# Two-layer hybrid trunk: the FFN up-projections take both activation parts behind one weight part

## The chip, the cores and the metric

The kernel runs on one core of one Trainium2 chip. The metric is the time of the program on the device in microseconds (us): the median of several runs. One more run is profiled; its trace gives the start and length of every instruction on the engines: TensorE (PE, and PEld for its weight loads), VectorE (DVE), ScalarE (ACT), GpSimd (POOL), and SyncE (SP), whose queue issues the large transfers.

## The reference

The input x is 256 tokens of 1024 channels in float32. Two layers follow one another, each of three steps:

```python
for l in range(DEPTH):                                   # DEPTH = 2
    x = x + 0.5 * swiglu(rms_norm(x, norm_gain[l, 0]), w_ffn_in[l, 0], w_ffn_out[l, 0])
    x = x + hybrid_mixer(rms_norm(x, norm_gain[l, 1]), ...)
    x = x + 0.5 * swiglu(rms_norm(x, norm_gain[l, 2]), w_ffn_in[l, 1], w_ffn_out[l, 1])

def swiglu(h, w_in, w_out):
    gate, up = jnp.split(h @ w_in, 2, axis=-1)           # 1024 -> 2 x 2816
    return (jax.nn.silu(gate) * up) @ w_out              # 2816 -> 1024
```

So there are four feed-forward networks (FFNs) and two mixers. The mixer (four kinds of attention, gates and an output projection) is not touched.

## The kernel before, in words

**Precision.** Every large product is made from split operands. A float32 weight is split into a high part (whi, a cast on ACT, line 187) and the rest (wlo, a subtraction on VectorE or, in a few places, on GpSimd, line 188), both in the type fp32r. The activations are split the same way; their two parts are hh and hl. A product is then three matmuls (mm3, lines 192 to 194): high by high, high by low, low by high.

**An FFN.** Its 2816 gate columns and 2816 up columns are done in 11 blocks j of 256 and 256. Blocks 0 and 1 go through up_first, where the tokens are stationary. Blocks 2 to 10 go through up(j, rv): the weight is stationary and the 256 tokens stream. In up, c counts the two halves of 128 columns, g is 0 for gate and 1 for up, and the 8 steps k run over the 1024 channels. One k-step is one mm3. For one c, the gate goes into the first 256 columns of a PSUM bank pm and the up values into the other 256. Then line 288 multiplies the whole bank by rb (the inverse norm of each token, in all partitions), line 291 takes SiLU of the gate half, line 293 multiplies, and lines 295 and 296 split the result into act for the down product.

After up(j) follow the down products of the rows m = 2j-4 and 2j-3: 12 matmuls of 512 columns for each m, into four accumulators that stay in PSUM over the FFN. The last four m are done in join, which also begins the next part of the layer (its norm, its first splits and transposes, the latter into banks pt).

**Order.** Raw weights come by SP's queue in tiles of 1 MB (five buffers) and are split into eight pairs of buffers in turn ("wide"); a split waits until its pair is free. The order of the instructions on each engine is set by a scheduler, which simulates the program, except in join, where it is fixed by hand, and for a few transfers that keep their place. One thing falls into the first FFN alone: setup, called behind block 3, builds the table of position biases (ld, then rep, 4 MB, then bias), with three transfers that stand in SP's queue among the weight loads.

Of the kernel before, what the change touches and what calls it, by code (L numbers as in the profile page):

```python
# [9 lines left out]
F32 = mybir.dt.float32  # L10
F32R = mybir.dt.float32r
AF = mybir.ActivationFunctionType
ALU = mybir.AluOpType
# [55 lines left out]
def tile_trunk(ctx: ExitStack, tc: tile.TileContext, a: dict, out: bass.AP):  # L69
# [49 lines left out]
    def norm(l, n):  # L119


        hh = h_p.tile([128, KC, T], F32R, name="hh", tag="hh")
        hl = h_p.tile([128, KC, T], F32R, name="hl", tag="hl")
        rs = sm.tile([128, 16], F32, name="rt", tag="rt", bufs=2)
        rb = wk.tile([128, T], F32, name="rb", tag="rb", bufs=1)

        def main(i):
            xg = []
            for q in range(2):
                ps = pt.tile([128, 4, 128], F32, name="pt", tag="pt")  # L130
                for c in range(4):
                    nc.tensor.transpose(ps[:, c, :], x[:, i, (4 * q + c) * 128:(4 * q + c + 1) * 128], ident[:])
                xg.append(wk.tile([128, 4, 128], F32, name="xg", tag="pT"))
                g = gn[:, 3 * l + n, 4 * q:4 * q + 4].rearrange("p (c o) -> p c o", o=1)
                nc.vector.tensor_tensor(xg[q][:], ps[:], g.to_broadcast([128, 4, 128]), op=ALU.mult)
                nc.scalar.copy(hh[:, 4 * q:4 * q + 4, i * 128:i * 128 + 128], xg[q][:])
            for q in range(2):
                o = (slice(None), slice(4 * q, 4 * q + 4), slice(i * 128, i * 128 + 128))
                nc.vector.tensor_tensor(hl[o], xg[q][:], f(hh[o]), op=ALU.subtract)  # L139

        def stats(i):
            ss = sm.tile([128, 16], F32, name="ss", tag="ss")
            for h in range(2):
                junk = wk.tile([128, 512], F32, name="junk", tag="e", bufs=3)
                nc.scalar.activation(out=junk[:], in_=x[:, i, h * 512:(h + 1) * 512], func=AF.Square,
                                     scale=D ** -0.5, accum_out=ss[:, h:h + 1])
            ms = sm.tile([128, 16], F32, name="ms", tag="ms")
            nc.vector.scalar_tensor_tensor(out=ms[:, 0:1], in0=ss[:, 0:1], scalar=EPS, in1=ss[:, 1:2],
                                           op0=ALU.add, op1=ALU.add)
            nc.gpsimd.tensor_tensor(rs[:, i:i + 1], ms[:, 0:1], neg_half[:, 0:1], op=ALU.pow)  # L150

        def rows():
            for i in range(NT):
                dg = wk.tile([128, 128], F32, name="dg", tag="av")
                nc.vector.tensor_scalar(out=dg[:], in0=ident[:], scalar1=rs[:, i:i + 1], scalar2=None, op0=ALU.mult)
                ps = pt.tile([128, 128], F32, name="pt", tag="pt")
                nc.tensor.matmul(ps[:], lhsT=ones[:], rhs=dg[:], start=True, stop=True)
                nc.scalar.copy(rb[:, i * 128:(i + 1) * 128], ps[:])

        return main, stats, (hh, hl, rs, rb, rows)  # L160

    def raw_tile(name="raw"):
        return raw_p.tile([128, 2048], F32, name=name, tag="raw")
# [27 lines left out]
    def mm3(ps, lh, ll, rh, rl, start, stop):  # L191
        nc.tensor.matmul(ps, lhsT=lh, rhs=rh, start=start, stop=False)  # L192
        nc.tensor.matmul(ps, lhsT=lh, rhs=rl, start=False, stop=False)  # L193
        nc.tensor.matmul(ps, lhsT=ll, rhs=rh, start=False, stop=stop)  # L194

    pinned = (mybir.EngineType.PE, mybir.EngineType.Activation, mybir.EngineType.DVE)

# [17 lines left out]
    def ffn(l, s, nxt=None, aside=None):  # L215
# [62 lines left out]

        def up(j, rv):
            for c in range(2):  # L280
                ps = pm.tile([128, 2, T], F32, name="pm", tag="pm")
                for g in range(2):
                    wh, wl = split(rv[g][:, :, c * 128:(c + 1) * 128], wide)
                    for k in range(KC):
                        mm3(ps[:, g, :], wh[:, k, :], wl[:, k, :], hh[:, k, :], hl[:, k, :],
                            k == 0, k == KC - 1)
                z = wk.tile([128, 2, T], F32, name="z", tag="pT")
                nc.vector.tensor_tensor(z[:], ps[:], rb[:].rearrange("p (o t) -> p o t", o=1)  # L288
                                        .to_broadcast([128, 2, T]), op=ALU.mult)
                sl = wk.tile([128, T], F32, name="sl", tag="sl")  # L290
                nc.scalar.activation(out=sl[:], in_=z[:, 0, :], func=AF.Silu)
                av = wk.tile([128, T], F32, name="av", tag="av")
                nc.vector.tensor_tensor(av[:], z[:, 1, :], sl[:], op=ALU.mult)
                ah, al = pair_tile()
                nc.scalar.copy(ah, av[:])  # L295
                nc.gpsimd.tensor_tensor(al, av[:], f(ah), op=ALU.subtract)  # L296
# [27 lines left out]
        w0, todo = first(0)  # L324
        w1, more = first(1)
        todo += more
        hh, hl, rs, rb, rows = yield todo
        yield from up_first(0, w0)
        rows()
        acc01 = pa.tile([128, 2, 512], F32, name="acc01", tag="a01")  # L330
# [121 lines left out]
    def mixer(l, nxt):  # L452
# [38 lines left out]
        g0, g1 = weights(804, 512, wide, (0, 1, 2, 3)), weights(0, 384, wide)  # L491
        w0, w1 = [], []
        todo = [lambda: w0.append(next(g0))] * 4 + [lambda: w1.append(next(g1))] * 4
        hh, hl, rt, rb, rows = yield todo
        ps0 = tiles()
        for i in range(NT):
            for e in range(4):
# [518 lines left out]
```

## Time and profile before

| what | value |
|---|---|
| median of 3 runs | 1394.11 us (1391.5 to 1396.48) |
| the profiled execution | 1394.26 us |
| its span, first to last instruction | 1392.5 us |
| granted TensorE clock, mean | 0.998 |
| PE busy | 1358.7 us, 98% |
| DVE busy | 875.7 us, 63% |
| ACT busy | 676.4 us, 49% |
| POOL busy | 265.0 us, 19% |
| chain that ended last, by engine | PE 91%, DVE 5%, ACT 2% |

How to read it: the share of PE says that TensorE does nearly all of the time; what an edit is worth is then how much it shortens the row of matmuls, less what it makes TensorE wait. The length shown for one matmul (0.28 us for 256 columns) covers its way through the pipeline; matmuls overlap, so their cost is the distance from one start to the next.

### The profile page before, as it was taken

What the parts mean: (1) busy time and instruction counts of PE and PEld (TensorE: products, weight loads), DVE (VectorE), ACT (ScalarE), POOL (GpSimd) and SP (SyncE); (2) the same over time, 40 slices, a digit from 0 to 9 for tenths busy, and PEclk for the clock granted to TensorE, in tenths of its full rate; (3) what the DMA queues carried; (4) which work ended last, traced back from release to release, by engine and by line L of the source; (5) the groups of instructions that cost most, each with busy time, mean ns of one, the idle gap of its engine ahead of it and who ended that gap; (6) DMA issues with size and microseconds to landing.
All of it is one profiled execution on the core that took longest, in us unless ns stands there. A gap on an engine that the chain in (4) does not pass through costs nothing.

```text
span 1392.5 us, 23262 instructions
## 1 busy us (share of the span) xinstructions
PE 1358.7 (98%) x9393; PEld 1254.2 (90%) x9393; DVE 875.7 (63%) x1498; ACT 676.4 (49%) x1052; POOL 265.0 (19%) x209
## 2 busy tenths in 40 slices
PE   7999999999999999999999999999999999999998
PEld 7998989879988989999999999898789989899997
DVE  6545646687587676555475555567866977765552
ACT  6424535646444555444454444355554555554441
POOL 0111232240022040111301111322300312211110
PEclk9999999999999999999999999999999999999999
DMA  9549733545343366555555555354543424665530
GB/s 348 173 157 372 252 118 120 186 149 180 122 143 101 122 213 210 182 182 182 182 177 187 182 182 197 95 168 156 182 136 122 152 91 146 212 209 190 183 122 31
DMA packets 173597, 237.10 MB, mean 170 GB/s; under 512 B 5085, under 2 KB 144545, under 8 KB 173489
## 3 DMA queue, kind: packets, MB, share of 16 engines
q1 hardware_dynamic: 172275, 235.16, 50.9%
q8 instruction: 74, 1.21, 0.3%
q10 hardware_dynamic: 1182, 0.38, 0.1%
q14 instruction: 34, 0.28, 0.1%
q0 software_dynamic: 32, 0.07, 0.0%
HBM read 234.51 MB, written 5.21 MB: 172 GB/s over the span
## 4 chain that ended last, share of the span: by engine, by line
PE 91%; DVE 5%; ACT 2%; issue 1%; DMA 1%; POOL 0%; SPq 0%; ACTq 0%; DVEq 0%; POOLq 0%
PE pm L192 17%; PE pm L194 17%; PE pm L193 17%; PE acc L192 6%; PE acc L193 6%; PE acc L194 6%; PE zp L193 4%; PE zp L194 4%; PE zp L192 4%; PE ov L586 2%; DVE wlo L188 2%; PE pt L579 1%; PE sl L811 1%; PE xo L194 1%; PE xo L193 1%
## 5 line engine op out<-in xcount | busy, mean ns | idle before, releaser
L188 DVE TENSOR_TENSOR wlo<-raw,whi 128x1024 fp32r<-128x1024 f32 (+3 forms) x426 | 514.6, 1213 | 275.1 <-ACT whi L187 272.9
L187 ACT CAST whi<-raw 128x1024 fp32r<-128x1024 f32 (+5 forms) x446 | 452.1, 1020 | 467.5 <-PE pm L193 293.8
L192 PE MATMUL pm<-hh,whi 128*128 128x256 f32 x1664 | 473.1, 284 | 3.2 <-ACT whi L187 1.9
L194 PE MATMUL pm<-hh,wlo 128*128 128x256 f32 x1664 | 472.6, 284 | 0.8 <-DVE wlo L188 0.8
L193 PE MATMUL pm<-hl,whi 128*128 128x256 f32 x1664 | 471.7, 283 | 0.0
L192 PEld LDWEIGHTS pm<-hh,whi 128*128 128x128 f32 x1664 | 317.1, 191 | 9.0 <-issue 4.6
L194 PEld LDWEIGHTS pm<-hh,wlo 128*128 128x128 f32 x1664 | 317.2, 191 | 2.9 <-issue 1.3
L193 PEld LDWEIGHTS pm<-hl,whi 128*128 128x128 f32 x1664 | 317.4, 191 | 1.7 <-issue 0.3
L296 POOL TENSOR_TENSOR act<-av,act 128x256 fp32r<-128x256 f32 x72 | 96.0, 1333 | 543.6 <-ACT act L295 539.2
L192 PE MATMUL acc<-whi,act 128*128 128x512 f32 x352 | 138.3, 394 | 0.0
L193 PE MATMUL acc<-wlo,act 128*128 128x512 f32 x352 | 138.2, 393 | 0.0
L194 PE MATMUL acc<-whi,act 128*128 128x512 f32 x352 | 137.9, 392 | 0.0
L193 PE MATMUL zp<-wlo,hh 128*128 128x512 f32 (+4 forms) x320 | 115.9, 363 | 1.1 <-DVE wlo L188 1.1
L194 PE MATMUL zp<-whi,hl 128*128 128x512 f32 (+4 forms) x320 | 114.4, 358 | 0.0
L192 PE MATMUL zp<-whi,hh 128*128 128x512 f32 (+4 forms) x320 | 110.1, 361 | 1.2 <-ACT whi L187 1.2
L288 DVE TENSOR_TENSOR z<-pm,rb 128x512 f32<-128x512 f32 x72 | 49.7, 691 | 57.0 <-PE pm L194 56.8
L906 POOL TENSOR_TENSOR yt<-yt,tg 128x512 f32<-128x512 f32 x24 | 40.9, 1725 | 204.7 <-DVE tg L904 198.0
L194 PEld LDWEIGHTS acc<-whi,act 128*128 128x128 f32 x352 | 66.1, 188 | 15.1
L192 PEld LDWEIGHTS acc<-whi,act 128*128 128x128 f32 x352 | 66.1, 188 | 13.3
L193 PEld LDWEIGHTS acc<-wlo,act 128*128 128x128 f32 x352 | 66.2, 188 | 13.1
L114 POOL TENSOR_TENSOR rs<-ms,neg_half 128x4 f32<-128x4 f32 (+3 forms) x44 | 53.5, 1223 | 124.9 <-DVE ms L111 124.9
L194 PE MATMUL pm<-whi,hl 128*128 128x256 f32 x256 | 73.0, 285 | 2.4 <-DVE hl L139 2.4
(189 smaller groups left out, 1790.5 us busy)
## 6 DMA issues: line engine op xcount, KB each, us to landing
raw<-in_w_ffn_in_dram SPq DMA_DIRECT2D x66, 1024.0 KB
raw<-in_w_in_dram SPq DMA_DIRECT2D x52, 1024.0 KB
raw<-in_w_ffn_out_dram SPq DMA_DIRECT2D x44, 1024.0 KB
raw<-in_w_ffn_in_dram SPq DMA_DIRECT2D x44, 512.0 KB
raw<-in_w_branch_dram SPq DMA_DIRECT2D x8, 1024.0 KB
raw<-in_w_out_dram SPq DMA_DIRECT2D x8, 1024.0 KB
raw<-in_w_in_dram SPq DMA_DIRECT2D x8, 768.0 KB
rep<-ld SPq DMA_DIRECT2D x1, 4032.0 KB
```

The source lines that it names most:

```text
L114: nc.gpsimd.tensor_tensor(rs[:, :n], ms[:, :n], neg_half[:, :n], op=ALU.pow)
L187: nc.scalar.copy(hv, src)
L188: (eng or nc.vector).tensor_tensor(lv, src, f(hv), op=ALU.subtract)
L192: nc.tensor.matmul(ps, lhsT=lh, rhs=rh, start=start, stop=False)
L193: nc.tensor.matmul(ps, lhsT=lh, rhs=rl, start=False, stop=False)
L194: nc.tensor.matmul(ps, lhsT=ll, rhs=rh, start=False, stop=stop)
L288: nc.vector.tensor_tensor(z[:], ps[:], rb[:].rearrange("p (o t) -> p o t", o=1) .to_broadcast([128, 2, T]), op=ALU.mult)
L296: nc.gpsimd.tensor_tensor(al, av[:], f(ah), op=ALU.subtract)
L579: nc.tensor.transpose(ps[:, c, :], p[:, (done + c) * 128:(done + c + 1) * 128], ident[:])
L586: nc.tensor.matmul(o[:, h, :], lhsT=pT[:, j, :], rhs=pv(j), start=j == 0, stop=j == nb - 1)
L811: nc.tensor.matmul(p, lhsT=q_of(h)[:, i * 128:(i + 1) * 128], rhs=k_of(h)[:, :n], start=True, stop=True)
L906: nc.gpsimd.tensor_tensor(y, y, t[:], op=ALU.add)
```

## The change

The two activation parts become the two halves of one tile h2. A k-step of up has two matmuls instead of three: the high weight part against both halves of h2 at once (512 columns, a whole bank), and the low weight part against the high half (256 columns, added into the first half of the bank). In the last step of a sum they are issued the other way round, so that the one that writes the whole bank ends it. Gate and up now have a bank each: the gate's from the pool pm, the up values' from the pool pt, which the transposes use as well. The two halves of a bank still have to be added. So for each of the two, the bank is multiplied into z (512 columns) and the halves of z are added (256 columns, both from SBUF). The gate is multiplied by rb, goes through SiLU, and is multiplied by rb again on GpSimd; the product is the factor of the up bank, which gives av.

```diff
--- before.py
+++ after.py
@@ -119,8 +119,8 @@
     def norm(l, n):
 
 
-        hh = h_p.tile([128, KC, T], F32R, name="hh", tag="hh")
-        hl = h_p.tile([128, KC, T], F32R, name="hl", tag="hl")
+        h2 = h_p.tile([128, 2, KC, T], F32R, name="h2", tag="h2")
+        hh, hl = h2[:, 0], h2[:, 1]
         rs = sm.tile([128, 16], F32, name="rt", tag="rt", bufs=2)
         rb = wk.tile([128, T], F32, name="rb", tag="rb", bufs=1)
 
@@ -157,7 +157,7 @@
                 nc.tensor.matmul(ps[:], lhsT=ones[:], rhs=dg[:], start=True, stop=True)
                 nc.scalar.copy(rb[:, i * 128:(i + 1) * 128], ps[:])
 
-        return main, stats, (hh, hl, rs, rb, rows)
+        return main, stats, (h2, rs, rb, rows)
 
     def raw_tile(name="raw"):
         return raw_p.tile([128, 2048], F32, name=name, tag="raw")
@@ -192,6 +192,14 @@
         nc.tensor.matmul(ps, lhsT=lh, rhs=rh, start=start, stop=False)
         nc.tensor.matmul(ps, lhsT=lh, rhs=rl, start=False, stop=False)
         nc.tensor.matmul(ps, lhsT=ll, rhs=rh, start=False, stop=stop)
+
+    def mm2(ps, wh, wl, r2, start, stop):
+
+
+        parts = [lambda: nc.tensor.matmul(ps, lhsT=wh, rhs=r2, start=start, stop=stop),
+                 lambda: nc.tensor.matmul(ps[:, 0], lhsT=wl, rhs=r2[:, 0], start=False, stop=False)]
+        for p in reversed(parts) if stop else parts:
+            p()
 
     pinned = (mybir.EngineType.PE, mybir.EngineType.Activation, mybir.EngineType.DVE)
 
@@ -278,19 +286,27 @@
 
         def up(j, rv):
             for c in range(2):
-                ps = pm.tile([128, 2, T], F32, name="pm", tag="pm")
+                ps = []
                 for g in range(2):
+                    pool, tag = (pm, "pm") if g == 0 else (pt, "pt")
+                    ps.append(pool.tile([128, 2, T], F32, name=tag, tag=tag))
                     wh, wl = split(rv[g][:, :, c * 128:(c + 1) * 128], wide)
                     for k in range(KC):
-                        mm3(ps[:, g, :], wh[:, k, :], wl[:, k, :], hh[:, k, :], hl[:, k, :],
-                            k == 0, k == KC - 1)
-                z = wk.tile([128, 2, T], F32, name="z", tag="pT")
-                nc.vector.tensor_tensor(z[:], ps[:], rb[:].rearrange("p (o t) -> p o t", o=1)
-                                        .to_broadcast([128, 2, T]), op=ALU.mult)
-                sl = wk.tile([128, T], F32, name="sl", tag="sl")
-                nc.scalar.activation(out=sl[:], in_=z[:, 0, :], func=AF.Silu)
-                av = wk.tile([128, T], F32, name="av", tag="av")
-                nc.vector.tensor_tensor(av[:], z[:, 1, :], sl[:], op=ALU.mult)
+                        mm2(ps[g][:], wh[:, k, :], wl[:, k, :], h2[:, :, k, :], k == 0, k == KC - 1)
+
+                def both(g, by, name):
+
+                    z = wk.tile([128, 2, T], F32, name="z", tag="pT")
+                    nc.vector.tensor_tensor(z[:], ps[g][:], by[:].rearrange("p (o t) -> p o t", o=1)
+                                            .to_broadcast([128, 2, T]), op=ALU.mult)
+                    r = wk.tile([128, T], F32, name=name, tag=name)
+                    nc.vector.tensor_tensor(r[:], z[:, 0], z[:, 1], op=ALU.add)
+                    return r
+
+                sl = both(0, rb, "sl")
+                nc.scalar.activation(out=sl[:], in_=sl[:], func=AF.Silu)
+                nc.gpsimd.tensor_tensor(sl[:], sl[:], rb[:], op=ALU.mult)
+                av = both(1, sl, "av")
                 ah, al = pair_tile()
                 nc.scalar.copy(ah, av[:])
                 nc.gpsimd.tensor_tensor(al, av[:], f(ah), op=ALU.subtract)
@@ -324,7 +340,8 @@
         w0, todo = first(0)
         w1, more = first(1)
         todo += more
-        hh, hl, rs, rb, rows = yield todo
+        h2, rs, rb, rows = yield todo
+        hh, hl = h2[:, 0], h2[:, 1]
         yield from up_first(0, w0)
         rows()
         acc01 = pa.tile([128, 2, 512], F32, name="acc01", tag="a01")
@@ -491,7 +508,8 @@
         g0, g1 = weights(804, 512, wide, (0, 1, 2, 3)), weights(0, 384, wide)
         w0, w1 = [], []
         todo = [lambda: w0.append(next(g0))] * 4 + [lambda: w1.append(next(g1))] * 4
-        hh, hl, rt, rb, rows = yield todo
+        h2, rt, rb, rows = yield todo
+        hh, hl = h2[:, 0], h2[:, 1]
         ps0 = tiles()
         for i in range(NT):
             for e in range(4):
```

On TensorE, in the second FFN, at the end of one g and the start of the next in block 2, before:

```order
L192 MATMUL pm_5882<-hh_5526,whi_5883 128x256
L193 MATMUL pm_5882<-hl_5527,whi_5883 128x256
L194 MATMUL pm_5882<-hh_5526,wlo_5884 128x256
L192 MATMUL pm_5882<-hh_5526,whi_5911 128x256
L193 MATMUL pm_5882<-hl_5527,whi_5911 128x256
L194 MATMUL pm_5882<-hh_5526,wlo_5912 128x256
```

and in the changed kernel the end of the first g, and then the start of the second (acc are the accumulators of the down products, act the activations):

```order
L200 MATMUL pm_5681<-h2_5326,wlo_5683 128x256
L199 MATMUL pm_5681<-h2_5326,whi_5682 128x512
L200 MATMUL pm_5681<-h2_5326,wlo_5683 128x256 x2
L199 MATMUL pm_5681<-h2_5326,whi_5682 128x512
L192 MATMUL acc01_5552<-whi_5793,act_5370 128x512
L193 MATMUL acc01_5552<-wlo_5794,act_5370 128x512
L194 MATMUL acc01_5552<-whi_5793,act_5370 128x512
```

```order
L193 MATMUL acc01_5552<-wlo_5810,act_5371 128x512
L281 MATMUL pt_5670<-ident_89,av_5668 128x128 x2
L199 MATMUL pt_5702<-h2_5326,whi_5703 128x512
L200 MATMUL pt_5702<-h2_5326,wlo_5704 128x256
L199 MATMUL pt_5702<-h2_5326,whi_5703 128x512
```

The three matmuls have become two, and in this block, which follows up_first and its transposes, one down product (12 matmuls) and the first two matmuls of the next have moved between the two g. In the later blocks nothing stands between them.

On VectorE, in the second FFN in block 4 (z is a bank times rb or sl; sl and av are the two halves of z added, or av the product of before), before:

```order
L288 TENSOR_TENSOR z_6279<-pm_6222,rb_5529 128x512
L188 TENSOR_TENSOR wlo_6488<-raw_6390,whi_6487 128x1024
L293 TENSOR_TENSOR av_6283<-z_6279,sl_6281 128x256
L188 TENSOR_TENSOR wlo_6527<-raw_6524,whi_6526 128x1024
L288 TENSOR_TENSOR z_6345<-pm_6288,rb_5529 128x512
L188 TENSOR_TENSOR wlo_6543<-raw_6524,whi_6542 128x1024
L293 TENSOR_TENSOR av_6349<-z_6345,sl_6347 128x256
```

and in the changed kernel:

```order
L300 TENSOR_TENSOR z_6019<-pm_5977,rb_5328 128x512
L303 TENSOR_TENSOR sl_6021<-z_6019 128x256
L188 TENSOR_TENSOR wlo_6182<-raw_6121,whi_6181 128x1024
L300 TENSOR_TENSOR z_6025<-pt_5998,sl_6021 128x512
L303 TENSOR_TENSOR av_6027<-z_6025 128x256
L188 TENSOR_TENSOR wlo_6203<-raw_6123,whi_6202 128x1024
L300 TENSOR_TENSOR z_6074<-pm_6032,rb_5328 128x512
L303 TENSOR_TENSOR sl_6076<-z_6074 128x256
L188 TENSOR_TENSOR wlo_6238<-raw_6235,whi_6237 128x1024
L300 TENSOR_TENSOR z_6080<-pt_6053,sl_6076 128x512
```

For each c there are a z and an add more, and one split stands between the first add and the second z, where ACT's SiLU and the product on GpSimd fall.

On SP's queue, in the first FFN (ld, rep and bias are the three transfers of setup; a pair of raw loads from w_ffn_in is one g of a block), before:

```order
L404 DMA ld_788<-line_786 21x384
L409 DMA rep_790<-ld_788 2688x1x384
L233 DMA raw_1202<-in_w_ffn_in_dram 128x4x256 x2
L313 DMA raw_1337<-in_w_ffn_out_dram 128x2x1024
L233 DMA raw_1371<-in_w_ffn_in_dram 128x4x256 x2
L233 DMA raw_1374<-in_w_ffn_in_dram 128x4x256 x2
L411 DMA bias_101<-rep_790 128x21x256
```

and in the changed kernel:

```order
L421 DMA ld_743<-line_741 21x384
L426 DMA rep_745<-ld_743 2688x1x384
L241 DMA raw_1113<-in_w_ffn_in_dram 128x4x256 x2
L329 DMA raw_1226<-in_w_ffn_out_dram 128x2x1024
L241 DMA raw_1260<-in_w_ffn_in_dram 128x4x256 x2
L428 DMA bias_101<-rep_745 128x21x256
L241 DMA raw_1263<-in_w_ffn_in_dram 128x4x256 x2
```

The transfer of bias has moved ahead of the second g of block 7; ld and rep keep their place in the queue.

## Rows read from the trace of the kernel before

**Rows 1.** Page: each engine's busy time with instructions, and the chain by engine.

```profile
PE 1358.7 (98%) x9393; PEld 1254.2 (90%) x9393; DVE 875.7 (63%) x1498; ACT 676.4 (49%) x1052; POOL 265.0 (19%) x209
PE 91%; DVE 5%; ACT 2%; issue 1%; DMA 1%; POOL 0%; SPq 0%; ACTq 0%; DVEq 0%; POOLq 0%
```

**Rows 2.** Page, costliest groups: count | busy us, mean ns | idle before, releaser.

```profile
L192 PE MATMUL pm<-hh,whi 128*128 128x256 f32 x1664 | 473.1, 284 | 3.2 <-ACT whi L187 1.9
```

**Rows 3.** Windows, first and second FFN: us; busy PE PEld DVE ACT POOL; PEclk, DMA, GB/s.

```profile
36.22:126.36 90.14, 87.50 (x613) 80.95 (x611) 47.15 (x66) 35.34 (x52) 9.50 (x9) 1.00 0.63 211
...
537.91:697.79 159.88, 159.88 (x1115) 149.36 (x1114) 86.52 (x94) 69.81 (x94) 34.42 (x22) 1.00 0.56 186
```

**Rows 4.** Timeline of PE, second FFN (start us, us): group starts in up and down.

```profile
555.12 0.28 PE L192 MATMUL pm<-hh,whi 128*128 128x256 f32 x1
...
557.93 0.28 PE L192 MATMUL pm<-hh,whi 128*128 128x256 f32 x1
...
560.81 0.28 PE L192 MATMUL pm<-hh,whi 128*128 128x256 f32 x1
...
566.50 0.40 PE L192 MATMUL acc<-whi,act 128*128 128x512 f32 x1
...
569.25 0.39 PE L192 MATMUL acc<-whi,act 128*128 128x512 f32 x1
...
571.97 0.28 PE L192 MATMUL pm<-hh,whi 128*128 128x256 f32 x1
...
588.94 0.28 PE L192 MATMUL pm<-hh,whi 128*128 128x256 f32 x1
...
600.43 0.40 PE L192 MATMUL acc<-whi,act 128*128 128x512 f32 x1
...
603.24 0.39 PE L192 MATMUL acc<-whi,act 128*128 128x512 f32 x1
...
605.99 0.28 PE L192 MATMUL pm<-hh,whi 128*128 128x256 f32 x1
```

**Rows 5.** Timeline of PE, mixer of layer 0: a plain run of 512 columns.

```profile
207.24 0.39 PE L192 MATMUL zp<-whi,hh 128*128 128x512 f32 x1
...
209.99 0.71 PE L132 MATMUL pt<-ident,x 128*128 128x128 f32 x5
```

**Rows 6.** Groups by line and shape, second FFN, 549.59 to 697.79 us, columns as above.

```profile
L188 DVE TENSOR_TENSOR wlo<-raw,whi 128x1024 fp32r<-128x1024 f32 x47 | 57.6, 1225 | 48.6 <-ACT whi L187 48.6
L187 ACT CAST whi<-raw 128x1024 fp32r<-128x1024 f32 x51 | 53.5, 1049 | 77.2 <-PE pm L193 53.5 <-PE acc L194 21.0 <-PE acc L193 2.6
...
L296 POOL TENSOR_TENSOR act<-av,act 128x256 fp32r<-128x256 f32 x18 | 24.9, 1385 | 128.8 <-ACT act L295 128.8
...
L288 DVE TENSOR_TENSOR z<-pm,rb 128x512 f32<-128x512 f32 x17 | 11.8, 692 | 13.8 <-PE pm L194 13.8
...
L293 DVE TENSOR_TENSOR av<-z,sl 128x256 f32<-128x256 f32 x17 | 9.2, 542 | 0.7 <-ACT sl L291 0.7
L291 ACT ACTIVATE sl<-z 128x256 f32<-128x256 f32 x17 | 7.0, 413 | 0.0
```

**Rows 7.** Timeline of DVE and POOL around 190 and 580 us (idle before, releaser).

```profile
190.20 2.52 DVE L293 TENSOR_TENSOR av<-z,sl 128x256 f32<-128x256 f32 x1 [0.66 <-ACT sl L291]
...
580.07 0.42 DVE L293 TENSOR_TENSOR av<-z,sl 128x256 f32<-128x256 f32 x1
...
190.03 2.41 POOL L188 TENSOR_TENSOR wlo<-raw,whi 128x1024 fp32r<-128x1024 f32 x1
...
193.24 0.74 POOL L296 TENSOR_TENSOR act<-av,act 128x256 fp32r<-128x256 f32 x1 [0.80 <-ACT act L295]
```

**Rows 8.** Timeline of SP's queue and of ACT in the first FFN, 79 to 114 us.

```profile
81.50 20.26 SPq L233 DMA_DIRECT2D raw<-in_w_ffn_in_dram  x2
...
110.63 1.96 SPq L411 DMA_DIRECT2D bias<-rep  x1
...
109.97 3.89 ACT L187 CAST whi<-raw 128x1024 fp32r<-128x1024 f32 x4 [12.85 <-DMA raw<-in_w_ffn_in_dram]
```

## The prediction

> **What bounds the kernel now.** I read the page first: TensorE is busy for 98% of the span and carries 91% of the chain that ended last [rows 1]. So the question at each place is whether TensorE waits there and for whom, and, where it doesn't wait, how long one of its instructions is. The up-projections of the feed-forward blocks (FFNs) are the largest group: of the three matmuls of their k-step each is there 1664 times, and the first of them waited 3.2 us in the whole run, 1.9 of it for a split weight [rows 2]. Next come the windows by stage. In a middle stretch (the second FFN) TensorE is busy for all of its 159.88 us; in the first FFN it is busy for 87.50 of 90.14, so it stood still there for 2.6 us [rows 3]. Last, the timeline of TensorE gives the pitch of its matmuls from start to start, which is what counts; the 0.28 us shown for one is its length in the pipeline. The granted clock is 1.00 in both windows, the 2.4 GHz level [rows 3], and nothing in the change should lower it, since TensorE stays as full.
>
> From [rows 4]: two up blocks of 96 matmuls of 256 columns take 566.50 - 555.12 = 11.38 and 600.43 - 588.94 = 11.49 us, so one takes (11.38 + 11.49) / 192 = 119.1 ns. Two pieces of down-projection, 24 matmuls of 512 columns each, take 5.47 and 5.56 us, 229.8 ns for one. One block with its down products takes 16.85 to 17.05 us, 16.95 in the mean. A plain run of twelve 512-column matmuls in the mixer takes 2.75 us, 229.2 ns each [rows 5].
>
> **Part 1, the matmuls.** The change removes from each k-step one 256-column matmul and its weight load and joins the other two that share a weight into one of 512 columns. Before, a k-step is 3 x 119.1 = 357.3 ns; after, it is 229.2 + 119.1 = 348.3, a saving of 9.0 ns. It is so small because the columns that stream stay the same (768); only the fixed part of one matmul goes, which the rows put at 2 x 119.1 - 229.2 = 9.0 ns. The bounds come from the fastest and slowest groups. Groups of 24 up matmuls take 2.81 us (557.93 - 555.12, 117.1 ns) or 2.88 (560.81 - 557.93, 120 ns). Groups of 12 down matmuls take 2.72 (571.97 - 569.25, 226.7 ns) or 2.81 (603.24 - 600.43, 234 ns) [rows 4]. All fast: 357.3 - 226.7 - 117.1 = 13.5 ns saved; all slow: 357.3 - 234 - 120 = 3.3. I take 9.0, from the run in which nothing but 512 columns differs.
>
> There are 9 blocks of 32 k-steps in each of 4 FFNs, 1152 k-steps. In the three later FFNs TensorE does not wait, so 27 x 32 = 864 steps give 864 x 9.0 = 7.8 us (2.9 to 11.7). In the first FFN the last four blocks run after the stall: 128 x 9.0 = 1.15 us (0.4 to 1.7). Its first five blocks come before or in the stall of 2.6 us, which is a wait for weights: ACT stands for 12.85 us until a raw weight lands at 109.97, since that transfer was issued at 81.50 [rows 8], right behind the replication of the bias table (rep, 4 MB, the row ahead of it in SP's order). What TensorE saves there, 160 x 9.0 = 1.4 us, lengthens that wait unless the table's transfers are issued earlier too. They are set off by work between the blocks before, which moves up with TensorE, so part is kept. Between 0 and 1.4 (all of it) I take 0.7.
>
> **Part 2, the bias transfer.** In the changed order the third of the table's transfers (2.75 MB, 110.63 before [rows 8]) goes ahead of the second weight half of block 7. At the mean rate of that stage, 211 GB/s [rows 3], it takes 13 us and the 1 MB behind it another 5, which lands near 128 us. By the pitches above that half is wanted some 6 us after block 6's last up matmul, near 126. So 0 to 2 us are lost; I take 0, since the mean holds the slow replication, and keep 2 for the range.
>
> **Part 3, the evacuation.** Each half block now needs two multiplies out of PSUM (0.692 us each [rows 6]), two adds of halves (0.42 as the old av without a collision [rows 7]; its mean with collisions is 0.542 [rows 6]), and a multiply on GpSimd of the size of L296, 0.74 us alone [rows 7] and 1.385 in the mean [rows 6]. Before, it was one multiply and one av. VectorE's work in a block goes from 6 x 1.225 + 2 x 0.692 + 2 x 0.42 = 9.6 us to 6 x 1.225 + 4 x 0.692 + 4 x 0.42 = 11.8, of 16.95 - 32 x 0.009 = 16.66 that TensorE takes. So 4.9 us stay free in a block. Collisions add to that: an av that met a split on GpSimd took 2.52 us instead of 0.42 [rows 7]. If all four GpSimd operations of a block (0.74 each) block VectorE in full, it is 14.8 us, still under 16.66. The Trainium skill ("SBUF — State Buffer", Who interferes with whom) states the same: a VectorE operation with two SBUF inputs and a GpSimd read shut each other out, one with a single SBUF input does not; by it the new adds collide and the multiplies out of PSUM do not, and the trace agrees (2.52 us beside 2.41).
>
> That VectorE and ACT are ahead is seen in the releaser of ACT's casts: of 77.2 us of waiting 53.5 ended when an up matmul freed a slot, none when a load came [rows 6]. So a chain that gets longer is covered by split weights in stock, at no cost to TensorE. The chain's own length decides only at two ends. The banks: g=1 now uses the pool of the transposes, each bank is wanted again two groups (2 x 2.8 us) after its last matmul, and reading it out needs 0.692 after at most one split (1.225); for g=1 the SiLU (0.413 [rows 6]) and the GpSimd multiply have the length of a group, 2.8 us, to finish. The last product of an FFN: block 10's last activation is wanted after 24 down matmuls and three pieces of six, (24 + 18) x 0.23 = 9.7 us. It needs 0.692 + 0.42 + a cast of about 0.4 + 1.4 on GpSimd, behind at most one or two GpSimd splits of 2.41 [rows 7] = 5.3 to 7.7 us. Both fit: 0. If the cover at the ends were gone, each us counts once per FFN.
>
> Block 2 of each later FFN runs in another order (one down product and two matmuls of the next ahead of the first g=1, as the change's rows show), 14 x 0.23 = 3 us, so the splits of those products are wanted about that much sooner. I put it at 0 as the splits there stand in stock, and at up to 0.7 for each of three FFNs in the range.
>
> **Sum.** 7.8 + 1.15 + 0.7 = 9.65 us, with ends 2.9 + 0.4 - 2 - 2 = -0.7 and 11.7 + 1.7 + 1.4 = 14.8. The profiled execution took 1394.26 (span 1392.5 [rows 1]), 0.15 above the median of the runs, which changes nothing: 1394.26 - 9.65 = 1384.6.
>
> **Rivals.** *A joined matmul costs almost its two halves.* If the 512-column matmul runs as in the slow down group (234 ns) beside slow 256-column ones (120), a step saves 3.3 ns and the sum is (864 + 128 + 80) x 3.3 = 3.5 us: 1390.8, no change that can be told. For it: the moving operand is now two separate stretches of 256 columns, and most down groups are not the fast ones. Against it: the mixer's 229.2 [rows 5]. The Trainium skill ("TensorE: Matmul & The Clock Gate", Wait — 56ns, not 53.3ns?) goes further: it puts the fixed cost of a back-to-back matmul at about 2.5 ns, so one removed would be worth 2.5 ns x 1072 = 2.7 us, 1391.6, on the same side. The rows disagree with 2.5 ns, as 9.0 stands there.
>
> *VectorE becomes the bound (the other side).* It runs in order. The second multiply waits for SiLU and the GpSimd multiply, and the splits stand behind it. If each of the two waits of a block costs it 0.41 + 0.74 + about 0.35 of hand-overs = 1.5 us, and every GpSimd operation blocks it, a block takes 14.8 + 3.0 = 17.8 us, above TensorE's 16.66; from there TensorE runs at VectorE's pace once the stock is used. Without any stock that is 27 x (17.8 - 16.95) = +23 us, 1417; with half of it covered, 1405. It decides from 16.66 us of VectorE in a block. Against it: in the changed order a split stands between the first add and the second multiply in every half block, which fills the wait, and the stock is several groups of 2.8 us.
>
> *More than the forecast.* If joined matmuls run at the fast rates only (13.5 ns a step) and the table's transfers move up in full: 1152 x 13.5 = 15.6 us, 1378.7. For it: fewer instructions and weight loads; against it: nothing shows why all groups should be fast.
>
> **How the numbers follow.** Forecast 0.67 (1384.6, between 1381 and 1389.5); joined matmul dear 0.16; VectorE the bound 0.08; more gain 0.09. What a measurement of this kernel can tell from no change is 0.3%, 4.2 us. Below 1389.9 is faster: 0.67 + 0.09 less a little of the forecast's upper end = 0.75; same, the dear joined matmul and that end, 0.17; slower 0.08. The range takes in the larger gain and most of the dear joined matmul: 1377 to 1393, which leaves out VectorE as the bound and the outer ends of the two neighbours.
>
> **What would show it.** Right: the starts in a middle up block come at 229 and 119 ns in turn and a block with its down products takes about 16.66 us; TensorE busy for all of the second FFN's window; VectorE near 70% there. Wrong: joined matmuls of 234 ns or more, or waits of TensorE for L188 splits, for a bank (L300) or for the last activations. In the first FFN the stall before block 6's weights should be longer than 2.6 us by about 0.7, and none should stand at block 7. The forecast fails if k-steps save under 4 ns or if TensorE waits over 5 us in the later FFNs.

## The result and the profile after

The changed kernel takes 1385.95 us (median of 4 runs, 1385.28 to 1388.2), the kernel before 1393.98 (1391.5 to 1396.48) in the same comparison, 8.0 us less, which is a ratio of 0.9942 between the two medians; the ratio on record is 0.9933, 95% interval 0.9921 to 0.9944. The forecast was 1384.6, 9.65 less than the profiled execution of before.

The profiled execution of after is the longest of the four (1388.2, span 1386.4), so the two traces stand 6.1 us apart and not 8.0. The first lines of its page, with the engines of [rows 1], and the new matmul and GpSimd groups beside [rows 2] (count | busy us, mean ns | idle before, releaser):

```profile
PE 1351.8 (98%) x8241; PEld 1195.4 (86%) x8241; DVE 951.3 (69%) x1642; ACT 687.5 (50%) x1052; POOL 337.3 (24%) x281
...
L199 PE MATMUL pt<-h,whi 128*128 128x512 f32 x576 | 210.5, 399 | 2.9 <-ACT whi L187 2.9
L199 PE MATMUL pm<-h,whi 128*128 128x512 f32 x576 | 208.5, 396 | 0.0
L308 POOL TENSOR_TENSOR sl<-sl,rb 128x256 f32<-128x256 f32 x72 | 82.9, 1151 | 326.1 <-ACT sl L307 324.6
```

The 1152 matmuls less are there (9393 to 8241), VectorE and GpSimd have more to do (875.7 to 951.3 and 265.0 to 337.3 us), and TensorE waited 2.9 us for the high part of an up weight in the whole run, all of it at one place, which is shown below. To see what a k-step is worth, take a stretch without any wait: in the second FFN the first down matmul behind block 3 and the one behind block 10, seven blocks apart. The timeline of before (the first of these rows is in [rows 4], at 566.50) and then that of after:

```profile
685.28 0.40 PE L192 MATMUL acc<-whi,act 128*128 128x512 f32 x1
```

```profile
565.85 0.40 PE L192 MATMUL acc<-whi,act 128*128 128x512 f32 x1
...
683.11 0.40 PE L192 MATMUL acc<-whi,act 128*128 128x512 f32 x1
```

685.28 - 566.50 = 118.78 us before, 683.11 - 565.85 = 117.26 after: 1.52 us on 7 x 32 = 224 k-steps, 6.8 ns each. The same seven blocks give 1.52 in the third FFN and in the fourth. The starts in between, worked out from the timelines: all 512-column up matmuls of that stretch stand 233.7 ns from the next start in the mean, the 256-column ones 117.2. That is a k-step of 350.9 ns where the prediction had 229.2 + 119.1 = 348.3; before, three matmuls of 119.2 make 357.7 in the same stretch.

With the same reading the two traces split as follows (starts of down matmuls; the last column is the prediction's term):

| stretch | before | after | difference | predicted |
|---|---|---|---|---|
| start to the first down matmul behind block 6, first FFN | 120.83 | 121.67 | +0.84 | -0.7 |
| from there to the one behind block 10 | 67.82 | 66.84 | -0.98 | -1.15 |
| from there to the end (mixers and three FFNs) | 1203.83 | 1197.93 | -5.90 | -7.8 |
| span | 1392.48 | 1386.44 | -6.04 | -9.65 |

The first line is the place where the changed kernel came out behind. The windows there, before and then after (us, busy time of PE, PEld, DVE, ACT, POOL, granted clock, DMA share, GB/s):

```profile
105.00:110.00 5.00, 4.18 (x30) 3.76 (x28) 0.00 (x0) 0.03 (x1) 0.00 (x0) 1.00 1.02 344
110.00:114.00 4.00, 2.17 (x16) 1.97 (x17) 2.95 (x4) 4.00 (x5) 0.00 (x0) 1.00 1.06 384
114.00:118.00 4.00, 4.00 (x36) 4.00 (x35) 4.00 (x6) 2.39 (x4) 0.00 (x0) 1.00 1.07 370
```

```profile
105.00:110.00 5.00, 2.63 (x16) 2.06 (x14) 0.00 (x0) 0.54 (x1) 0.00 (x0) 1.00 0.97 346
110.00:114.00 4.00, 2.69 (x10) 2.09 (x11) 3.46 (x5) 4.00 (x6) 0.27 (x1) 0.84 1.07 367
114.00:118.00 4.00, 4.00 (x19) 3.46 (x18) 4.00 (x4) 1.90 (x3) 2.98 (x2) 0.74 1.10 359
```

TensorE stood still for 0.82 + 1.83 = 2.65 us before and for 2.37 + 1.31 = 3.68 after. And after, the granted clock then fell to 0.84 and 0.74 of full in the means of the next two windows (in steps of 2 us from 112 it reads 0.68, 0.50 and 0.97; 0.50 is the 1.2 GHz level), which costs (1 - 0.84) x 4 + (1 - 0.74) x 4 = 1.7 us. Before, 2.65 us of standing still was not followed by a fall. Why the wait grew is read from the queue and from ACT, with [rows 8]; after:

```profile
78.54 0.88 SPq L426 DMA_DIRECT2D rep<-ld  x1
79.59 21.38 SPq L241 DMA_DIRECT2D raw<-in_w_ffn_in_dram  x2
...
109.46 1.04 ACT L187 CAST whi<-raw 128x1024 fp32r<-128x1024 f32 x1 [14.47 <-DMA raw<-in_w_ffn_in_dram]
```

The weight load's issue stood in SP's queue for 21.38 us (20.26 before). It began 1.9 us earlier but the weight landed only 0.5 us earlier (109.46 against 109.97), while TensorE came there 1.5 us earlier (it stopped at 107.63 against 109.18). The landing differs between executions by as much: two more traces of the same order, below, have it at 108.20 (contig) and 109.76 (a_again). TensorE stood still for 3.75 and 3.25 us in these, so the size of the growth, 1 us here, is in part chance.

The kernel's executions differ by such falls of the clock. Both of these traces have two more in the mixers (near 356 and 1040 us), so these two cancel; the traces of other runs lack one of them, or have one elsewhere (contig near 294 us). Without the 1.7 us of the fall at 112 the two traces would stand 7.7 us apart, near the 8.0 of the medians. Whether a fall follows is not settled by the length of the waits alone: in the first mixer (near 353 us in both) TensorE stands still for 1.03 and 0.72 us in the trace of every run here, and the fall behind that is in those of before, after, a_again and contig, but not in those of zigzag or actq_a.

### The profile page after: what moved, and what is told of

The parts are those of the page before. It is cut to its first block, busy times and chain, and to the rows that moved or that the text cites. A ratio compares the mean times of both kernels' runs of the same rounds, so it can differ in the third digit from the quotient of the medians.

```text
span 1386.4 us, 21269 instructions
## 1 busy us (share of the span) xinstructions
PE 1351.8 (98%) x8241; PEld 1195.4 (86%) x8241; DVE 951.3 (69%) x1642; ACT 687.5 (50%) x1052; POOL 337.3 (24%) x281
## 4 chain that ended last, share of the span: by engine, by line
PE 90%; DVE 5%; ACT 2%; issue 1%; DMA 1%; POOL 1%; SPq 0%; ACTq 0%; DVEq 0%; POOLq 0%
PE pt L199 9%; PE pm L199 9%; PE pm L192 7%; PE pm L194 7%; PE pm L193 7%; PE acc L192 6%; PE acc L193 6%; PE acc L194 6%; PE pt L200 5%; PE pm L200 5%; PE zp L193 4%; PE zp L194 4%; PE zp L192 4%; PE ov L604 2%; DVE wlo L188 2%
## 5 line engine op out<-in xcount | busy, mean ns | idle before, releaser
L199 PE MATMUL pt<-h,whi 128*128 128x512 f32 x576 | 210.5, 399 | 2.9 <-ACT whi L187 2.9
L199 PE MATMUL pm<-h,whi 128*128 128x512 f32 x576 | 208.5, 396 | 0.0
L200 PE MATMUL pt<-h,wlo 128*128 128x256 f32 x576 | 150.5, 282 | 0.8 <-DVE wlo L188 0.8
L200 PE MATMUL pm<-h,wlo 128*128 128x256 f32 x576 | 149.6, 280 | 0.0
L192 PE MATMUL pm<-h,whi 128*128 128x256 f32 x512 | 148.0, 289 | 1.3 <-DVE tg L922 1.3
L194 PE MATMUL pm<-h,wlo 128*128 128x256 f32 x512 | 147.1, 287 | 0.0
L193 PE MATMUL pm<-h,whi 128*128 128x256 f32 x512 | 146.8, 287 | 0.0
L199 PEld LDWEIGHTS pt<-h,whi 128*128 128x128 f32 x576 | 109.0, 189 | 22.9 <-ACT whi L187 3.2
L199 PEld LDWEIGHTS pm<-h,whi 128*128 128x128 f32 x576 | 108.2, 188 | 20.8 <-issue 0.6
L312 POOL TENSOR_TENSOR act<-av,act 128x256 fp32r<-128x256 f32 x72 | 83.4, 1159 | 165.3 <-ACT act L311 157.5
L193 PE MATMUL zp<-wlo,h 128*128 128x512 f32 (+4 forms) x320 | 115.9, 363 | 1.1 <-DVE wlo L188 1.1
L200 PEld LDWEIGHTS pt<-h,wlo 128*128 128x128 f32 x576 | 109.4, 190 | 7.3 <-DVE wlo L188 1.1
L194 PE MATMUL zp<-whi,h 128*128 128x512 f32 (+4 forms) x320 | 114.4, 358 | 0.0
L192 PE MATMUL zp<-whi,h 128*128 128x512 f32 (+4 forms) x320 | 110.1, 361 | 1.2 <-ACT whi L187 1.2
L192 PEld LDWEIGHTS pm<-h,whi 128*128 128x128 f32 x512 | 97.7, 191 | 5.3 <-issue 4.3
```

Source lines behind the costliest of these rows:

```text
L199: parts = [lambda: nc.tensor.matmul(ps, lhsT=wh, rhs=r2, start=start, stop=stop), lambda: nc.tensor.matmul(ps[:, 0], lhsT=wl, rhs=r2[:, 0] ...
L200: lambda: nc.tensor.matmul(ps[:, 0], lhsT=wl, rhs=r2[:, 0], start=False, stop=False)]
```

## The experiments

**The changed kernel again, and the joining undone.** The ratios below are each to runs of the kernel before on the same chip.

> The changed kernel once more, as the measure for the others and for a second trace. Theory (the clock dip behind the stall in the first FFN is not in every execution): about 1386 us; if the trace has no dip below 1.00 between 105 and 125 us, its span is about 1.5 to 2 us shorter than the 1386.4 of the first trace. Rival (the gap between the traces and the medians lies elsewhere): the stall and the dip look the same and the span is again 1386.4.

Measured: 1387.12 us, ratio 0.9946 (0.9931 to 0.9962). The trace has the stall (TensorE stood still for 3.25 us) and the fall of the clock again, and the fall lasts twice as long; its span is 1387.7. So the theory that a second trace would lack the fall did not hold for this run. Its six executions range from 1385.46 at a mean granted clock of 0.997 to 1389.42 at 0.995, those of before beside them from 1391.14 at 1.000 to 1398.4 at 0.994: at like clocks (0.995 and 0.996, the two that both kernels show) they stand 7.7 and 7.6 us apart.

```diff
     def mm2(ps, wh, wl, r2, start, stop):
+        if not (start or stop):
+            for i, w, r in ((0, wh, 0), (1, wh, 1), (0, wl, 0)):
+                nc.tensor.matmul(ps[:, i], lhsT=w, rhs=r2[:, r], start=False, stop=False)
+            return
```

> The changed kernel with the joining undone in six of the eight k-steps of a sum (three matmuls of 256 columns into the same bank, as before); banks, adds and order of the evacuation stay. Theory (the gain is the fixed part of the matmul that is saved, the evacuation is hidden): a k-step of the later FFNs goes back from about 352 to 357 or 358 ns in six of eight, so 864 x 6 = 5.2 us later in FFNs 2 to 4 and up to 1 us in the first, 1391 to 1392. Rival (the longer evacuation costs TensorE time that the joining pays back): slower than the kernel before, 1396 or more, with waits of TensorE in the trace.

Measured: 1394.01 us, ratio 0.9994 (0.9984 to 1.0005). With six of eight joinings undone nearly the whole gain is gone, and the kernel with all of the longer evacuation is not slower than the one before. The second FFN of un_join, 549 to 690 us, in windows, and the same seven blocks:

```profile
549.00:690.00 141.00, 141.00 (x950) 130.20 (x950) 96.10 (x119) 66.72 (x87) 41.71 (x34) 1.00 0.58 193
```

```profile
570.95 0.40 PE L192 MATMUL acc<-whi,act 128*128 128x512 f32 x1
...
689.27 0.40 PE L192 MATMUL acc<-whi,act 128*128 128x512 f32 x1
```

TensorE is busy for all 141.00 us beside VectorE's 96.10. Seven blocks take 118.32 us, 0.46 less than before; a quarter of 1.52, for the quarter of k-steps that stay joined, is 0.38. So the gain is the joining's and the evacuation costs TensorE nothing here. The time was 2 us over what was expected, since the first FFN's stall was longer in this order (TensorE stood still for 5.3 us, with a fall of the clock that goes on behind it).

**Why 234 ns and not 229.** Three guesses on the joined matmul. First the layout:

```diff
-        h2 = h_p.tile([128, 2, KC, T], F32R, name="h2", tag="h2")
+        h2 = h_p.tile([128, KC, 2, T], F32R, name="h2", tag="h2")
```

> The changed kernel with the tile of the two activation parts laid out so that the 512 columns of a joined matmul lie in one stretch. Theory A (the joined matmul's 234 ns, 5 over the mixer's plain run, come from its two stretches of 256): pitch of the joined ones 229 to 230, time down by 1152 x 4.5 = 5 us to about 1381. Theory B (the pitch comes from the change of size from one matmul to the next, or from where the weights lie): pitch 233 to 235 still, time 1386 within 1 us.

Measured: 1387.29 us, ratio 0.9947 (0.9933 to 0.996), as the changed kernel beside it. The seven blocks take the same 117.26 us:

```profile
565.81 0.40 PE L192 MATMUL acc<-whi,act 128*128 128x512 f32 x1
...
683.07 0.40 PE L192 MATMUL acc<-whi,act 128*128 128x512 f32 x1
```

Two stretches of 256 columns cost no more than one of 512. This kernel's instructions stand in the same order as the changed kernel's, and its trace has no fall of the clock at 112 us. Its weight landed 1.3 us earlier, TensorE stood still for as long, 3.75 us, but in three pieces between 107 and 118 us (1.61, 0.76 and 1.39), and the first down matmul behind block 6 started at 120.45 instead of 121.67. Then the order in a k-step:

```diff
-        for p in reversed(parts) if stop else parts:
+        for p in reversed(parts) if odd else parts:
...
-                        mm2(ps[g][:], wh[:, k, :], wl[:, k, :], h2[:, :, k, :], k == 0, k == KC - 1)
+                        mm2(ps[g][:], wh[:, k, :], wl[:, k, :], h2[:, :, k, :], k == 0, k == KC - 1, k % 2)
```

> The changed kernel with the two matmuls of every second k-step in reversed order, so that joined ones stand next to joined ones (512, 256, 256, 512, 512, 256, ...). Theory B1 (a matmul of 512 columns followed by one of 256 costs some ns more): the joined ones that are followed by a joined one are back at 229, the pair of steps is 2 x 5 x 1/2 = 5 ns shorter, time down by about 2 to 3 us. Theories A and B2 (two stretches, or where the weights lie): pitches 234 and 118 in any order, 1386 within 1 us.

Measured: 1384.9 us, ratio 0.9931 (0.9914 to 0.9947), 2.2 us under the changed kernel beside it, though the intervals overlap. The trace is clearer:

```profile
563.25 0.39 PE L192 MATMUL acc<-whi,act 128*128 128x512 f32 x1
...
680.12 0.39 PE L192 MATMUL acc<-whi,act 128*128 128x512 f32 x1
```

116.87 us for the seven blocks, 0.39 less, or 1.7 ns a k-step (0.31 and 0.39 in the third and fourth FFN). The order is worth that much, but not in the way that was expected: the joined matmuls that are followed by a joined one did not go back to 229. They stand at 232.8 ns, and those followed by a 256-column one at 232.9; the joined ones came down by 0.9 ns in the mean (to 232.8) and the 256-column ones by 0.6 (to 116.6). So this run does not show that the change of size is what costs. The third guess was the buffers:

```diff
-    wide = own + [("cq", "ck"), ("dq", "dk"), ("dv", "bqk"), ("aqk", "br"), ("xn", "xn")]
+    wide = [("xn", "xn"), ("aqk", "br"), ("dv", "bqk"), ("dq", "dk"), ("cq", "ck")] + own[::-1]
```

> The changed kernel with the eight pairs of weight buffers taken in reversed turn. Theory C (the pitch of a joined matmul, 224 to 241 ns in repeating patterns, comes from which buffer holds its weights): at the same place of the program the patterns are others than in the changed kernel. Rival (the pattern comes from the place in the program): at the same place of the second FFN the same patterns, for instance 224, 233, 241, 235 in the second group of block 3. The time is 1386 within 2 us in both.

Measured: 1389.53 us in a single run, above the 1386 within 2 us that was expected. The distances from start to start (ns) of the joined matmuls in the second group of block 3, worked out from the timelines:

```
changed kernel   235 224 233 241 235 232 241
buffers reversed 235 230 228 230 228 230 229
```

At the same place of the program the pattern is another one, so it goes with the buffers that hold the weights, or with what comes with them, and not with the place. In both kernels the patterns also come back four blocks later, which is 24 splits or three rounds of the eight pairs. The seven blocks of the third FFN take 117.35 us against 117.16, but that sum hides two things: the joined matmuls came down from 233.6 to 232.3 ns in the mean (256-column ones from 117.2 to 117.0), and the 168 down matmuls in between, whose weights lie in the same buffers, went up from 229.7 to 232.7. So the buffers alone move the k-step by about as much as the reversed order does. What in a buffer makes 224 or 241 ns was not found.

**Where VectorE would begin to decide.**

```diff
-        for p in reversed(parts) if stop else parts:
+        for p in reversed(parts) if stop else parts[:1]:
```

> The changed kernel without the products of the low weight part in up, except in the last step of each sum (7 of 8 are left out): TensorE's block falls to 24 x 0.2298 + 32 x 0.234 + 4 x 0.118 = 13.5 us, while VectorE, ACT, GpSimd and the transfers have what they had. Theory (VectorE's work of a block is 11.3 us and its waits are covered): TensorE stays busy in the second FFN, a block takes 13.5 us. Rival (with its in-order waits VectorE needs 14.8 to 17.8 us for a block): blocks of 14.8 us or more, TensorE waiting for L188 splits or for a bank. With seven bits of 118 ns left out, 512-column matmuls stand next to each other: their pitch is 229 if the change of size costs the rest, 234 if it does not.

Measured: 1286.76 us in a single run. In the second FFN six blocks, from 560.32 to 640.55, take 13.37 us each, with TensorE busy throughout and VectorE at 82% of the window. One wait shows up at the end of that FFN (who waited, for whom, then us, times and the longest):

```profile
560.00:641.00 81.00, 81.00 (x365) 66.56 (x364) 66.11 (x86) 46.90 (x61) 30.63 (x25) 1.00 0.72 246
```

```profile
560.32 0.40 PE L192 MATMUL acc<-whi,act 128*128 128x512 f32 x1
...
640.55 0.40 PE L192 MATMUL acc<-whi,act 128*128 128x512 f32 x1
```

```profile
PE acc L194 <- POOL act L312: 1.5, 1, 1.5
```

The rival with 14.8 to 17.8 us of VectorE in a block falls: 13.37 us are enough for it, so the 16.75 of a block of the changed kernel (117.26 / 7) leave room. The wait for L312 is the last activation of the FFN, late by 1.5 us once the blocks are 3.4 us shorter; the changed kernel has no such wait. (In the first FFN of this run TensorE waits 15.7 us for a weight, so its time as a whole says little.) Next to each other the 512-column up matmuls stand 230.1 (bank pt) and 230.9 ns (pm) apart in the mean, most of the way from 234 to 229. The turn of the buffers is that of the changed kernel, so it goes with the missing 256-column matmuls, be it as neighbours of another size or by their weight loads; these two were not told apart.

**The stall of the first FFN.** The theory was that weights come late because the table's replication (rep) stands ahead of them. First it was moved behind block 6, in the changed kernel (late_a), in the kernel before (late_b), and in the changed kernel with the reversed order (best):

```diff
-            if aside and j == 3:
+            if aside and j == 6:
```

> The changed kernel with the table of position biases built behind block 6 of the first FFN instead of block 3, when more split weights are in stock. Theory (the first FFN's share of the gain goes into the wait for block 6's weights behind the table's transfers, and into a clock dip after it): no wait of TensorE between 105 and 125 us, no dip there, time down by the 3.7 us of waits and up to 1.7 us of the dip, to about 1382. Rival (the transfers stall the weights wherever they stand): the wait moves to about 150 us, time within 1 us of 1386 to 1387.

> The kernel before with the same move of the table, to see what the change is worth without that wait. Theory: down by about 2.6 us from the kernel before, so that the pair late_a and late_b stands 9 us or more apart (1152 steps x 7 ns = 8 us, and the dip). Rival: no change from the kernel before, and the pair 8 us apart as the two kernels are.

> The table behind block 6 and the reversed order in every second k-step together. If both gains stand by themselves: about 1.5 to 2 us below late_a (a pair of matmuls 350.2 instead of 351.9 ns over 1152 steps), near 1380. If the reversed order's gain was the stall and the dips of single executions only: the same as late_a within 1 us.

Measured: late_a 1389.95 us, ratio 0.9962 (0.995 to 0.9975); late_b 1401.15, ratio 1.0042 (1.0028 to 1.0055), slower than before; best 1387.35, ratio 0.9948 (0.9936 to 0.9961), 2.6 us under late_a. The rival held: the stall moved along. In late_a:

```profile
150.00:160.00 10.00, 7.80 (x38) 6.29 (x37) 0.00 (x0) 0.86 (x1) 0.00 (x0) 1.00 0.97 330
160.00:170.00 10.00, 7.82 (x29) 6.75 (x30) 9.16 (x12) 5.92 (x8) 3.22 (x2) 0.66 1.08 370
```

TensorE stands still for 2.2 + 2.2 us, which is one wait from 157.8 to 162.2, and the clock is at half for 6.8 us from 161.2 on, which costs about 2.9 us behind the wait. In late_b it stands still for 7.3 us in these windows. More weights in stock did not cover the 20 us in which SP's queue issued nothing. So the queue itself was taken next: rep goes out on ACT's queue, behind ACT's small loads, and its last transfer (bias) is called behind block 8.

```diff
-        tc.keep_in_program_order(nc.sync.dma_start(out=rep[:], in_=src))
+        tc.keep_in_program_order(nc.scalar.dma_start(out=rep[:], in_=src))
...
-            if aside and j == 3:
+            if aside and j in (3, 8):
```

> The changed kernel with the replication of the bias table (4 MB) issued on ACT's queue instead of SP's, and its last transfer later on SP's, so that no weight load stands behind the replication in a queue. Theory (weight loads wait 20 us in SP's queue behind the replication, and that is the stall of the first FFN wherever it is put): both kinds of transfer run at once, TensorE waits less than 1 us between 105 and 170 us, no dip there, time 3 to 5 us under the changed kernel, about 1382. Rival (the 16 DMA engines themselves are full with the replication): weights still come late, the stall is as long, 1386 to 1388.

> The kernel before with the same move of the replication to ACT's queue. Theory: down by its 2.6 us of waits there and a dip in some executions, to about 1392; the pair actq_a and actq_b stands 8.5 to 10 us apart, since 1152 steps then give their 7 ns without a wait that takes the first five blocks' share back. Rival: 1394 to 1396, and 8 us apart or less.

Measured: actq_a 1382.94 us, ratio 0.9917 (0.9903 to 0.9931); actq_b 1389.23, ratio 0.9962 (0.9948 to 0.9977). Both gain (1382 and 1392 were expected), and TensorE no longer waits from 100 to 180 us. The changed kernel with SP's queue blocked, and then actq_a:

```profile
85.00:105.00 20.00, 20.00 (x108) 17.07 (x107) 7.72 (x17) 3.64 (x6) 3.58 (x4) 1.00 0.60 204
```

```profile
80.00:105.00 25.00, 25.00 (x134) 21.32 (x133) 19.82 (x31) 12.42 (x17) 6.82 (x6) 1.00 0.80 260
105.00:126.00 21.00, 21.00 (x114) 18.04 (x113) 11.43 (x17) 6.84 (x10) 5.04 (x4) 1.00 0.64 226
126.00:140.00 14.00, 14.00 (x75) 11.97 (x74) 9.09 (x12) 6.23 (x9) 3.59 (x3) 1.00 1.08 376
```

Between 85 and 105 us the transfers now run at 256 GB/s (260 from 80 us on), where they ran at 204. So the stall was the blocked queue and not full DMA engines. Two things moved at once, though, and what the later bias transfer is worth by itself was not measured. The medians of the pair stand 6.3 us apart and not the 8.5 to 10 that were expected. In the traces, without the stall, the change gives 2.4 us in the first FFN (down matmul behind block 10 at 183.09 against 185.48) and 1.52 in seven blocks of each later one, as ever. The two traces stand 10.8 us apart, but that of actq_b has two falls of the clock more in the first mixer, 1.7 us each, which leaves 7.4. The executions of actq_b ran at mean clocks of 0.996 to 1.000, those of actq_a at 0.996 to 0.998. With four and five runs whose falls of the clock differ, the 6.3 is not told apart from 8.

**Both together.** Replication on ACT's queue, and the reversed order in every second k-step:

> The replication on ACT's queue and the reversed order in every second k-step together. If both hold by themselves: no wait of TensorE behind the replication, a pair of matmuls at about 350.2 ns instead of 351.9 over 1152 steps (2 us), so 7.3 us less than the kernel before for the changed k-step and the same 4 us for the stall: about 0.9905 of the kernel before, 1380 to 1382. If the reversed order is worth nothing beyond the stall: 0.9917 as with the replication alone.

Measured: 1379.66 us, ratio 0.9896 (0.9879 to 0.9912), the fastest here, 14.5 us under the kernel before. The reversed order was 2.2, 2.6 and 3.3 us faster in its three pairs (the last across two comparisons), and 1152 x 1.4 to 1.7 ns = 1.6 to 2.0 us of that is in the traces of the matmuls.

## Why the prediction held, and which terms were off

The direction, the mechanism and the time held: fewer fixed parts of matmuls, an evacuation that is hidden. The sum was 9.65 for a measured 8.0, with two terms too high. That the time came within 1.4 us is in part luck: at 6.8 ns a k-step all 1152 of them are worth 7.8 us, the first FFN's wait takes some of it back, and a single fall of the clock moves an execution by 1.7 us or more either way.

- **The k-step, 9.0 ns, is 6.8.** The step that failed is the choice of 229.2 for the joined matmul, from a run in which nothing but 512-column matmuls follow one another. In the k-step it stands between 256-column ones, and there it is 233.7: 4.5 ns more, just short of the 234 that the prediction named as a sign of being wrong. What kept the saving at 6.8 is an error the other way: the 256-column matmul, put at 119.1, is 117.2 beside joined ones. (The step before was 357.7, not 357.3, which makes up the rest.) Part of the 4.5 goes with the 256-column neighbours or their weight loads (230.1 to 230.9 without them), part with the buffers of the weights (232.3 in reversed turn, third FFN); reversing every second step gave back up to 1.7 ns of the k-step. The later FFNs gave 5.9 us of the predicted 7.8. The rival with 3.3 ns, all groups slow, had the joined matmul right and fell with its 120 for the 256-column ones.
- **The first FFN before its stall, -0.7, is +0.8 in the trace.** What TensorE saved became waiting, as the step said (3.68 us against 2.65, 1.0 longer where 0.7 was put), with the weight 0.5 us earlier. The wait is followed by a fall of the clock worth 1.7 us, which the prediction didn't have. Without that the line would be -0.9; the trace of contig, which has as much waiting and not the fall, reads 120.45, or -0.4.
- **Nothing for the bias transfer** held: TensorE is busy for all of 122 to 130 us after (the first half of that below), where the second half of block 7 was wanted, and the wait that it might have cost is not there:

```profile
122.00:126.00 4.00, 4.00 (x19) 3.28 (x18) 3.30 (x5) 1.57 (x4) 1.89 (x2) 1.00 1.05 405
```

- **Nothing for the evacuation** held, shown by un_join (ratio 0.9994 with all of it, and TensorE busy for all of the window) and no_wl. VectorE was put at 11.8 us a block; in the window of 141 us it is 95.21 us, 11.3 in a block. The GpSimd multiply took 1.15 us in the mean, not 0.74, as most of them meet a split on VectorE. The second z waits for it, 0.7 us each time by its row, and nobody waits for that:

```profile
549.00:690.00 141.00, 141.00 (x740) 120.30 (x739) 95.21 (x116) 67.62 (x85) 47.44 (x38) 1.00 0.57 190
```

```profile
L300 DVE TENSOR_TENSOR z<-pt,sl 128x512 f32<-128x512 f32 x18 | 12.5, 692 | 14.3 <-POOL sl L308 12.6 <-PE pt L199 1.7
```

The Trainium skill's 2.5 ns for a matmul's fixed part ("TensorE: Matmul & The Clock Gate", Wait — 56ns, not 53.3ns?) would have given 2.7 us in all; the seven blocks show 6.8 ns a k-step, so for these fp32r matmuls with a weight load each the rule does not fit.

What stays open: what in a weight buffer makes a 512-column matmul 224 or 241 ns, why it is dearer among 256-column ones, and how often the kernel's executions have the fall of the clock at 112 us (two of three traces of this order do).

## What to carry to other kernels

Joining two matmuls of the same weight saves only the fixed part of one, 6.8 ns a k-step here, so it pays where there are a thousand of them on an engine that never waits, and where the adding afterwards falls on an engine with room. Price a matmul by its distance to the next start among neighbours like those it will have, since the same 512 columns were 229 to 231 ns in their own kind and 234 among shorter ones. And before counting a saving ahead of a stall, look what sets the stall's end: here the weight waited in a queue behind a large transfer, and TensorE's coming 1.5 us earlier did not bring it as much earlier. Moving the large transfer (and its last part) was worth 4.5 us in the kernel before, more than half of what the change itself was worth.

## What the runs showed of the hardware

- SP issued no further transfer for some 20 us behind the 4 MB replication (20.26 us before, 21.38 after), while the DMA engines' busy share from 80 to 100 us was 0.41 and 0.46; issued from ACT's queue, the same replication ran beside the weight loads, and the stretch from 85 to 105 us went from 204 to 256 GB/s (actq_a).
- In the first FFN's stall TensorE's granted clock did not fall after waits of 1.89 + 0.76 us (before) or 1.61 + 0.76 and, 5.6 us later, 1.39 (contig). It fell to 0.50, the 1.2 GHz level, after 2.93 + 0.76 us (after; cost 1.7 us), during 2.78 + 0.46 (a_again) and during a single wait of 4.39 (late_a; cost about 2.9). So the longest single piece sorts these five and the total (3.75 without a fall, 3.25 with one) does not. It is no rule for the whole kernel: in the first mixer 1.03 + 0.72 us were followed by a fall in some traces (before, after) and not in others (zigzag, actq_a).
- The distance between starts of the same 512-column matmul varies from 224 to 241 ns in patterns that change with the turn of the weight buffers (slots_rev) and come back every four blocks; where the moving operand lies (one stretch or two) makes no difference (117.26 us for seven blocks in both).
